# Gate transposes moved to the head of the mLSTM, convolution norm made a step of its own, gate scratch in other buffers

## Chip, core and metric

One NeuronCore of a Trainium2 chip runs the whole program. Its engines are TensorE (PE, with its weight loads as PEld), VectorE (DVE), ScalarE (ACT), GpSimd (POOL) and SyncE (SP), which issues nearly all DMAs. The metric is the device time of one execution in microseconds.

## What is computed

Two layers over 256 latent tokens and 256 context tokens, model width 1024. Each layer has an attention part and an expert part (PEER); the change is in the attention part. Cut to what matters:

```python
h  = rmsnorm(x, norm1_g) * (1.0 + sc1) + sh1          # latent; context with its own modulation
a, mq, mk, mv, mo, mg, dq, dk, dv = split(h @ w_in)
conv  = conv_module(a)         # gate, depthwise convolution of 31 taps, layernorm over 256 channels, silu
mlstm = mlstm_mixer(mq, mk, mv, mo, mg)   # 4 heads, forward and backward, gated by mg
diff  = diff_mixer(dq, dk, dv)            # 4 heads, softmax(q1 k1) - lam * softmax(q2 k2)
x = x + g1 * (concat(conv, mlstm, diff) @ w_out)
x = x + g2 * peer_ffn(rmsnorm(x, norm2_g) * (1.0 + sc2) + sh2)
```

In the second layer the context tokens are needed as keys, values and gates only, so convolution, queries and outputs there cover 256 columns in place of 512.

## The kernel before

The features lie on the 128 partitions and the 512 tokens (context, then latent) on the free axis. `front` (from line 366) is the attention part of a layer, `peer` (from line 889) the expert part. All matrix products are made in three passes: weights and activations are split into a high and a low part. The split of weights (`wsplit`, L228 to L240) loads a block by DMA from SyncE's queue (L232, two buffers), makes the high part on ScalarE (L238) and the low part on GpSimd (L239), 512 columns at a time, into five buffers each.

The order of `front` in the first layer:
- two adaLN halves (`ada_half`, L199), the norm, and the first group projection (`projg`, L331 to L333), which gives the gates, and two blocks of the convolution's input;
- `gate_rows` (L510): on VectorE and ScalarE, logarithm, exponential, splits, cumulative sums (`scan`, L545 and L549) of the gates on 64 partitions. Results: `rows` (L561 to L563), read along the tokens, and ih, il, which are transposed (L569, eight transposes into one PSUM bank of tag "m"), copied to `ah` (L572, VectorE) and exponentiated to `ea` (L573, ScalarE);
- the convolution's gate, the output gates (L407), three late adaLN halves (`late`, L410: accumulators on VectorE, L145 and L147; row products on TensorE, L214; their weights w2 in the buffers kT and qT), the keys, queries and values of the mLSTM (L412 to L419);
- then the steps of `ORDER` (L37), for both layers `kmcvkk0k123`: "k" the keys and queries of one head pair of the differential attention (`keys`, L423, with a rotation through TensorE, L359), "m" the mLSTM (`mlstm`, L595), "c" the convolution with its norm (`conv`, L481), "v" the values of the attention (`values`, L432), digits one head of it (`diff`, L662);
- the output projection, residual and second norm.

`conv` is, for two blocks of 128 channels, one step L486 and thirty steps L489 on VectorE, and then the norm: the mean over 256 channels by two matmuls with ones (L493), VectorE's subtraction (L495), squares and their sum (`sumsq`, L268 and L269), reciprocal root (`rsqrt`, L256 to L261), scale, sigmoid and product (L501 to L506).

The head of `mlstm` spreads a row over the partitions (L611, PSUM tag "m"), and from it makes E by exponentials with bias `ah` on ScalarE (L619), on the diagonal blocks by VectorE's add and minimum with `ah` (L623), an exponential (L625) and GpSimd's triangle (L627); L632 is the product of keys and queries, L637 multiplies it by `ea` and E, L643 is the product with the values.

What sets the order: the program is written in the order told (the traced order). When it is built, a planner lays the instructions out on each engine by its own estimate of durations: among those that it takes to be ready it issues the one traced first, and one traced later may go ahead when the earlier isn't ready yet. On the chip every engine then takes its fixed list in order. `keep_in_program_order` binds an instruction behind the one traced before it on its engine, in order of issue alone. Tiles of one tag share that many buffers as `bufs` says: of the tags here "m" (PSUM) has two, "a" (PSUM) one, "f" (PSUM) three, "PT" two, "v", "vx", "kT" and "qT" one each. "PT" holds the accumulators of the adaLN halves, and later the transposed probabilities of `diff`.

Of the kernel before, what the change touches and what calls it, by code (L numbers as in the profile page):

```python
# [7 lines left out]
F32 = mybir.dt.float32  # L8
# [17 lines left out]
TT = 512  # L26
# [7 lines left out]
LAG = (10, 4)  # L34
HB = 1
LO = ('p', 'p')
ORDER = ('kmcvkk0k123', 'kmcvkk0k123')  # L37
NSUM = 4
MORE = (4, 6)
WB = 5  # L40
# [9 lines left out]
class Net:  # L50
# [315 lines left out]
    def front(self, l, P, c0, late):  # L366

        nc, I, F = self.nc, self.I, self.frontp
        n = TT - c0
# [12 lines left out]
        W = I["w_t"][l]  # L382
        K = self.K = {}
        first = self.projg(I["w_first"][l, 0], h, 0, ("f", "f", "f", "d"))
        rows = self.gate_rows(P, first[0], K)

        vx = K["vx"] = F.tile([128, 4, 4, 128], F32, name="vx", tag="vx")
        for hh in range(4):
# [2 lines left out]
        km = K["km"] = F.tile([128, 2, TT], F32, name="km", tag="km")  # L391
        mq = K["mq"] = F.tile([128, 2, n], F32, name="mq", tag="mq")
        og = K["og"] = F.tile([128, 2, n], F32, name="og")
        v = K["v"] = F.tile([128, 4, 512], F32, name="v", tag="v")
        up = F.tile([128, 2, ns, T + 30], F32, name="up")
        nc.gpsimd.memset(up[:, :, :, 0:15], 0.0)
        nc.gpsimd.memset(up[:, :, :, T + 15:T + 30], 0.0)
# [25 lines left out]
        def keys(b):  # L423
            pk = self.proj(W[BLK_DK + b], h, 0)
            nc.scalar.activation(kT[:, b, :T], pk[:, :T], AF.Copy)
            self.rot(pk[:, T:], kT[:, b, T:])
            pq = self.proj(W[BLK_DQ + b], h, c0)
            if c0 == 0:
                nc.scalar.activation(qT[:, b, :T], pq[:, :T], AF.Copy, scale=0.125)
            self.rot(pq[:, T - c0:TT - c0], qT[:, b, T - c0:], 0.125)  # L430

        def values():  # L432
            for k in range(2):
                for t2, p in enumerate(self.projv(I["w_v"][l, 1 + k], h)):
                    nc.scalar.activation(v[:, 2 * t2:2 * t2 + 2, 256 * k:256 * k + 256], p, AF.Copy)


        seen = 0
        for s in ORDER[l]:
            if s == "m":  # L440
                self.mlstm(P, K, rows, c0)
            elif s == "c":
                cy = self.conv(P, up, n)
            elif s == "v":
                values()
            elif s == "k":
                keys(seen)
                seen += 1
            else:
                self.diff(P, K, int(s), c0)  # L450
# [30 lines left out]
    def conv(self, P, up, n):  # L481
        nc = self.nc
        ys = [self.frontp.tile([128, n], F32, name=f"cy{b}") for b in range(2)]
        for b in range(2):
            y = ys[b].rearrange("p (s t) -> p s t", t=T)
            nc.vector.tensor_scalar(y, up[:, b, :, 0:T], P["conv_w"][:, b, 0:1], P["conv_b"][:, b:b + 1],  # L486
                              op0=OP.mult, op1=OP.add)
            for k in range(1, CONV_K):
                nc.vector.scalar_tensor_tensor(y, up[:, b, :, k:k + T], P["conv_w"][:, b, k:k + 1], y,  # L489
                                         op0=OP.mult, op1=OP.add)  # L490
        mu = self.ps("a")[:, :n]
        for b in range(2):
            nc.tensor.matmul(mu, self.ones, ys[b], start=b == 0, stop=b == 1)  # L493
        for b in range(2):
            nc.vector.scalar_tensor_tensor(ys[b], mu, -1.0 / 256.0, ys[b], op0=OP.mult, op1=OP.add)  # L495
        split = lambda t: t.rearrange("p (s t) -> p s t", t=T)
        yv = [split(y) for y in ys]
        sq, y = (up[:, b, :, 0:T] for b in range(2))
        rs = self.rsqrt(self.sumsq(yv, self.ones, split(self.ps("a")[:, :n]), [sq, y]), 1.0 / 256.0, y, sq)
        for b in range(2):  # L500
            nc.vector.tensor_mul(yv[b], yv[b], rs)  # L501
            nc.vector.tensor_scalar(ys[b], ys[b], P["conv_ln_g"][:, b:b + 1], P["conv_ln_b"][:, b:b + 1],
                                    op0=OP.mult, op1=OP.add)
            sg = self.w(n, "sg", fam="c")
            last = nc.scalar.activation(sg, ys[b], AF.Sigmoid)
            nc.vector.tensor_mul(ys[b], ys[b], sg)  # L506
        self.log_exp(last)
        return ys

    def gate_rows(self, P, ps, K):  # L510

        nc, F = self.nc, self.frontp
        T1 = F.tile([128, 4, TT], F32, name="gr1", tag="v")
        T2 = F.tile([64, 4, TT], F32, name="gr2", tag="vx")
        G = T1[:, 0]
        Fg, e, u = (T1[0:64, k] for k in (1, 2, 3))
        r, L, Bl, M = (T2[:, k] for k in range(4))
        nc.vector.tensor_scalar(G, ps, P["gate_b"][:, 0:1], None, op0=OP.add)
        nc.vector.tensor_copy(Fg, G[64:128])
        ig = G[0:64]  # L520
        nc.scalar.activation(e, Fg, AF.Abs)
        nc.scalar.activation(e, e, AF.Exp, scale=-1.0)
        nc.vector.tensor_scalar(u, e, 1.0, None, op0=OP.add)
        nc.scalar.activation(L, u, AF.Ln)
        nc.vector.tensor_scalar(r, u, -1.0, None, op0=OP.add)
        nc.vector.tensor_sub(r, e, r)
        nc.scalar.activation(u, L, AF.Exp, scale=-1.0)
        nc.vector.tensor_mul(r, r, u)
        nc.vector.tensor_add(L, L, r)
        nc.vector.scalar_tensor_tensor(L, Fg, 0.0, L, op0=OP.min, op1=OP.subtract)  # L530
        lh, ll, ih, il = e, u, r, Fg

        def split(hi, lo, v):
            nc.vector.tensor_scalar(hi, v, SPLIT, None, op0=OP.add)
            nc.vector.tensor_scalar(hi, hi, SPLIT, None, op0=OP.subtract)
            nc.vector.tensor_sub(lo, v, hi)
        split(lh, ll, L)
        split(ih, il, ig)

        def scan(dst, src, op):  # L540
            for d in range(2):
                p = slice(32 * d, 32 * d + 32)
                z = (lambda a: self.zero[p].to_broadcast([32, a.shape[1]])) if op == OP.add else (lambda a: a)
                if d == 0:
                    nc.vector.tensor_tensor_scan(dst[p], src[p], z(src[p]), 0.0, op0=op, op1=op)  # L545
                else:
                    for o, init in ((0, 0.0), (T, dst[p, 0:1])):
                        a = src[p, o:o + T][:, ::-1]
                        nc.vector.tensor_tensor_scan(dst[p, o:o + T][:, ::-1], a, z(a), init, op0=op, op1=op)  # L549
        Bh = L  # L550
        scan(Bh, lh, OP.add)
        scan(Bl, ll, OP.add)
        nc.vector.tensor_sub(ih, ih, Bh)
        nc.vector.tensor_sub(il, il, Bl)
        scan(M, ih, OP.max)
        out = T1[0:64, 2:4]
        nc.vector.tensor_scalar(out[:, 0], M, -1.0, None, op0=OP.mult)
        nc.vector.tensor_add(out[:, 1], Bh, M)
        nc.vector.tensor_add(out[:, 1], out[:, 1], Bl)
        nc.scalar.activation(out[:, 1], out[:, 1], AF.Exp, scale=-1.0)  # L560
        rows = F.tile([128, 2, TT], F32R, name="rows")  # L561
        nc.scalar.activation(rows[:64], out, AF.Copy)
        nc.vector.tensor_sub(rows[64:], out, rows[:64])  # L563
        K["ah"] = F.tile([128, 4, 64], F32, name="ah")
        K["ea"] = F.tile([128, 4, 64], F32, name="ea")
        pt = self.ps("m")
        for k, src in enumerate((ih, il)):
            for tt in range(4):
                nc.tensor.transpose(pt[:, (4 * k + tt) * 64:(4 * k + tt) * 64 + 64],  # L569
                                    src[:, tt * 128:(tt + 1) * 128], self.ident[:64, :64])  # L570
        pv = pt.rearrange("p (k t r) -> p k t r", k=2, t=4)
        nc.vector.tensor_copy(K["ah"], pv[:, 0])  # L572
        nc.scalar.activation(K["ea"], pv[:, 1], AF.Exp)  # L573
        return rows

    def spans(self, i, d, c0):

# [601 lines left out]
```

## Time and profile before

| what | us |
|---|---|
| median of 3 runs | 3153.36 (3150.83 to 3155.54) |
| the profiled execution | 3152.63 |
| its span, first to last instruction | 3150.9 |
| busy: TensorE, weight loads | 2936.4 (93%), 2428.7 (77%) |
| busy: VectorE | 2300.6 (73%) |
| busy: ScalarE, GpSimd | 1443.4 (46%), 1340.1 (43%) |
| mean granted clock of TensorE, share of full speed | 0.971 |

The share of busy time is a mean over stages that have different limits; what a change in one stage is worth is read in that stage. The first attention part lies at about 50 to 403 us of the span, the second at about 2054 to 2290 us. In a line, L569 is line 569 of the kernel, "m<-ident,gr" the tile written and the tiles read, "[8.63 <-DVE gr L553]" idle time of the engine just before, and whose work ended it.

### The profile page before, as it was taken

How to read it: one execution, taken by the hardware profiler on the slowest of the kernel's cores; microseconds unless marked ns; L12 is line 12 of the kernel's file. 1: busy time of each engine (PE TensorE's matmuls, PEld its weight loads, DVE VectorE, ACT ScalarE, POOL GpSimd, SP SyncE). 2: the span in 40 equal slices, each digit the busy share in tenths (PEclk: the TensorE clock that was granted, in tenths of full speed). 3: DMA queues.
4: the chain of work that ended last, by engine and by line, in shares of the span. 5: the costliest groups of instructions: out<-in, count | busy, mean ns of one | idle time of the engine just before them, and what ended most of it. 6: DMA issues, size and time to landing. Idle time of an engine off the chain costs nothing. (4 is left out here: it accounts for less than half of the span.)

```text
span 3150.9 us, 43726 instructions
## 1 busy us (share of the span) xinstructions
PE 2936.4 (93%) x14930; PEld 2428.7 (77%) x14930; DVE 2300.6 (73%) x4819; ACT 1443.4 (46%) x2863; POOL 1340.1 (43%) x1055
## 2 busy tenths in 40 slices
PE   7899989989999998889999999988988899899998
PEld 4476677778888876767888888777787899788887
DVE  7987649977777769997455545586669898766665
ACT  4345443336666632223333333345453666455554
POOL 3334244446666646343434334253466776000000
PEclk9999999999999999999999999999998999999999
DMA  6511123335555587776564645121255677887864
GB/s 223 174 48 54 47 87 115 127 110 201 202 206 204 201 286 247 232 242 198 164 189 152 194 148 173 41 75 60 74 162 162 210 269 261 302 273 250 269 224 139
DMA packets 249807, 550.96 MB, mean 175 GB/s; under 512 B 17440, under 2 KB 118304, under 8 KB 246384
## 3 DMA queue, kind: packets, MB, share of 16 engines
q1 hardware_dynamic: 248864, 545.74, 52.3%
q8 instruction: 118, 1.93, 0.2%
q0 software_dynamic: 720, 2.43, 0.2%
q14 instruction: 105, 0.86, 0.1%
HBM read 456.87 MB, written 91.23 MB: 174 GB/s over the span
## 5 line engine op out<-in xcount | busy, mean ns | idle before, releaser
L863 POOL TENSOR_TENSOR ul<-u,uh 128x512 fp32r<-128x512 f32 x448 | 593.5, 1334 | 433.7 <-ACT uh L862 423.1
L880 PE MATMUL h<-hh,uh 128*128 128x512 f32 (+1 forms) x2048 | 700.1, 342 | 36.1 <-ACT ga L886 34.8
L882 PE MATMUL h<-hh,ul 128*128 128x512 f32 (+1 forms) x2048 | 696.4, 340 | 3.9 <-POOL ul L863 3.9
L881 PE MATMUL h<-hl,uh 128*128 128x512 f32 (+1 forms) x2048 | 697.1, 340 | 0.0
L862 ACT ACTIVATE vh<-v 128x512 fp32r<-128x512 f32 x512 | 319.8, 629 | 573.9 <-PE acc L994 375.6
L862 ACT ACTIVATE uh<-u 128x512 fp32r<-128x512 f32 x512 | 318.8, 628 | 411.9 <-PE h L881 293.5
L863 POOL TENSOR_TENSOR vl<-v,vh 128x512 fp32r<-128x512 f32 x208 | 303.7, 1473 | 365.5 <-ACT vh L862 361.2
L880 PEld LDWEIGHTS h<-hh,uh 128*128 128x128 f32 x2048 | 395.8, 193 | 79.6 <-ACT ga L886 37.4
L882 PEld LDWEIGHTS h<-hh,ul 128*128 128x128 f32 x2048 | 395.2, 193 | 45.9 <-POOL ul L863 4.4
L881 PEld LDWEIGHTS h<-hl,uh 128*128 128x128 f32 x2048 | 395.9, 193 | 38.8
L993 PE MATMUL acc<-vl,wh 128*128 128x512 f32 x1024 | 402.9, 393 | 3.2 <-DVE vl L863 2.9
L992 PE MATMUL acc<-vh,wh 128*128 128x512 f32 x1024 | 402.2, 393 | 3.0 <-ACT vh L862 3.0
L994 PE MATMUL acc<-vh,wl 128*128 128x512 f32 x1024 | 401.4, 392 | 0.0
L831 DVE TENSOR_REDUCE rt_stg<-f 128x256 f32<-128x512 f32 x384 | 243.5, 686 | 142.1 <-PE f L829 141.1
L239 POOL TENSOR_TENSOR wlo<-wt,whi 128x512 fp32r<-128x512 f32 x164 | 242.7, 1491 | 245.3 <-ACT whi L238 217.8
L958 DVE TENSOR_TENSOR ga<-ga,g 128x512 f32<-128x512 f32 x192 | 164.7, 863 | 165.9 <-DMA ga<-act 102.2
L863 DVE TENSOR_TENSOR vl<-v,vh 128x512 fp32r<-128x512 f32 x304 | 208.3, 701 | 105.5 <-ACT vh L862 105.1
L992 PE MATMUL f<-vh,wh 128*128 128x512 f32 x512 | 205.1, 401 | 37.3 <-DVE accS L1000 31.2
L1000 DVE TENSOR_TENSOR accS<-accS,f 128x512 f32<-128x512 f32 x252 | 171.1, 679 | 85.2 <-PE f L994 85.1
L993 PEld LDWEIGHTS acc<-vl,wh 128*128 128x128 f32 x1024 | 194.2, 190 | 46.8 <-DVE vl L863 6.8
L992 PEld LDWEIGHTS acc<-vh,wh 128*128 128x128 f32 x1024 | 193.9, 189 | 43.7 <-ACT vh L862 3.2
L994 PEld LDWEIGHTS acc<-vh,wl 128*128 128x128 f32 x1024 | 193.9, 189 | 40.4
(318 smaller groups left out, 5393.3 us busy)
## 6 DMA issues: line engine op xcount, KB each, us to landing
u<-in_peer_u SPq DMA_DIRECT2D x256, 512.0 KB, 4.0
v<-in_peer_v SPq DMA_DIRECT2D x256, 512.0 KB, 4.4
G<-rt_stg SPq DMA_DIRECT2D x24, 2048.0 KB, 7.0
act<-ga SPq DMA_DIRECT2D x152, 256.0 KB, 2.9
ga<-act SPq DMA_DIRECT2D x152, 256.0 KB, 4.5
g<-G SPq DMA_DIRECT2D x32, 1024.0 KB, 6.1
wa<-in_ada_t SPq DMA_DIRECT2D x56, 512.0 KB, 4.2
w<-in_ada_w SPq DMA_DIRECT2D x20, 1024.0 KB, 6.2
```

The costliest lines, as they stand in the source:

```text
L239: nc.gpsimd.tensor_sub(lo, raw, hi)
L831: nc.vector.tensor_reduce(stg[:, :, t4 + k2:t4 + k2 + 2].rearrange("p j t -> p t j"), pg.rearrange("p (t x j) -> p t j x", t=2, x=2), axis ...
L862: nc.scalar.activation(hi, raw[:, k * 512:(k + 1) * 512], AF.Copy)
L863: lo_eng.tensor_sub(lo, raw[:, k * 512:(k + 1) * 512], hi)
L880: nc.tensor.matmul(o, uh, hh[:, c, c0:], start=c == 0, stop=False)
L881: nc.tensor.matmul(o, uh, hl[:, c, c0:], start=False, stop=False)
L882: nc.tensor.matmul(o, ul, hh[:, c, c0:], start=False, stop=c == NB - 1)
L958: nc.vector.tensor_mul(av, av, g)
L992: nc.tensor.matmul(A, wh[:, t], vh, start=s0 and jj == 0, stop=False)
L993: nc.tensor.matmul(A, wh[:, t], vl, start=False, stop=False)
L994: nc.tensor.matmul(A, wl[:, t], vh, start=False, stop=s1 and jj == 1)
L1000: nc.vector.tensor_add(o, o, A)
```

## The change

- `gate_rows` ends with `rows` and hands back ih and il; their transposes, `ah` and `ea` become a function `gate_cols`, called at the start of the step "m". Each transpose is bound behind what was traced before it on TensorE, so behind the second rotation of the first "k".
- The norm becomes a function `conv_norm` and a step "n" of its own, after "v"; its two matmuls of the mean are bound behind the values' matmuls.
- The scratch of the gates: gr2 (tag "vx", four rows of 512) becomes gr2 and gr3 (tag "PT", two rows each); ih takes the row of Fg and il that of ig, both in gr1 (tag "v"), which so lives until the transposes. The value tile `v` of the attention, of the same tag, is allocated in its step.

```diff
-ORDER = ('kmcvkk0k123', 'kmcvkk0k123')
+ORDER = ('kmcvnkk0k123', 'kmcvnkk0k123')
...
-        rows = self.gate_rows(P, first[0], K)
+        rows, gates = self.gate_rows(P, first[0], K)
...
-        v = K["v"] = F.tile([128, 4, 512], F32, name="v", tag="v")
...
         def values():
+            v = K["v"] = F.tile([128, 4, 512], F32, name="v", tag="v")
...
             if s == "m":
+                self.gate_cols(K, gates)
                 self.mlstm(P, K, rows, c0)
             elif s == "c":
                 cy = self.conv(P, up, n)
+            elif s == "n":
+                self.conv_norm(P, up, n, cy)
...
+        return ys
+
+    def conv_norm(self, P, up, n, ys):
+        nc = self.nc
         mu = self.ps("a")[:, :n]
         for b in range(2):
-            nc.tensor.matmul(mu, self.ones, ys[b], start=b == 0, stop=b == 1)
+            self.tc.keep_in_program_order(nc.tensor.matmul(mu, self.ones, ys[b], start=b == 0, stop=b == 1))
...
-        T2 = F.tile([64, 4, TT], F32, name="gr2", tag="vx")
+        T2, T3 = (F.tile([64, 2, TT], F32, name=k, tag="PT", bufs=2) for k in ("gr2", "gr3"))
...
-        r, L, Bl, M = (T2[:, k] for k in range(4))
+        r, L, Bl, M = T2[:, 0], T2[:, 1], T3[:, 0], T3[:, 1]
...
-        lh, ll, ih, il = e, u, r, Fg
+        lh, ll, ih, il = e, u, Fg, ig
...
+        return rows, (ih, il)
+
+    def gate_cols(self, K, srcs):
+
+        nc, F = self.nc, self.frontp
         K["ah"] = F.tile([128, 4, 64], F32, name="ah")
         K["ea"] = F.tile([128, 4, 64], F32, name="ea")
         pt = self.ps("m")
-        for k, src in enumerate((ih, il)):
+        for k, src in enumerate(srcs):
             for tt in range(4):
-                nc.tensor.transpose(pt[:, (4 * k + tt) * 64:(4 * k + tt) * 64 + 64],
-                                    src[:, tt * 128:(tt + 1) * 128], self.ident[:64, :64])
+                self.tc.keep_in_program_order(
+                    nc.tensor.transpose(pt[:, (4 * k + tt) * 64:(4 * k + tt) * 64 + 64],
+                                        src[:, tt * 128:(tt + 1) * 128], self.ident[:64, :64]))
```

## Rows read from the trace of the kernel before

**Rows 1.** Busy time of each engine by stretch: start:end, length, then each engine.

```profile
core 0: us, PE busy (x) PEld busy (x) DVE busy (x) ACT busy (x) POOL busy (x), PEclk, DMA share, GB/s
76.00:183.50 107.50, 93.03 (x401) 58.77 (x402) 103.60 (x139) 33.35 (x56) 43.98 (x26) 0.95 0.45 152
104.00:110.00 6.00, 5.92 (x15) 2.33 (x16) 5.77 (x10) 0.38 (x1) 0.00 (x0) 0.50 0.11 20
2067.00:2135.60 68.60, 48.99 (x309) 43.30 (x308) 66.90 (x94) 30.80 (x57) 38.74 (x26) 0.89 0.26 85
2094.90:2100.00 5.10, 5.09 (x16) 3.65 (x17) 4.91 (x8) 0.00 (x0) 0.00 (x0) 0.50 0.01 3
2135.60:2142.00 6.40, 6.34 (x28) 5.86 (x28) 2.74 (x9) 2.31 (x7) 2.14 (x3) 0.58 0.01 3
...
183.50:235.00 51.50, 47.69 (x238) 34.97 (x238) 40.23 (x68) 24.36 (x56) 15.16 (x23) 0.90 0.09 31
```

**Rows 2.** TensorE's waits, total, times, longest: 76 to 183, 183 to 403, 2067 to 2142.

```profile
PE m L569 <- DVE gr L553: 8.6, 1, 8.6
...
PE m L632 <- DVE E L623: 1.7, 1, 1.7
...
PE f L349 <- POOL wlo L239: 1.0, 2, 0.7
...
PE m L569 <- DVE gr L553: 11.3, 1, 11.3
PE a L493 <- DVE cy L489: 6.7, 1, 6.7
```

**Rows 3.** VectorE's timeline, first layer: start, length, line, tiles, shapes, count.

```profile
64.55 0.47 DVE L145 TENSOR_SCALAR ada<-w,cc 128x512 f32<-128x512 f32 x1
...
69.06 7.16 DVE L147 SCALAR_TENSOR_TENSOR ada<-w,cc,ada 128x512 f32<-128x512 f32 x6
...
109.72 0.68 DVE L558 TENSOR_TENSOR gr<-gr 64x512 f32<-64x512 f32 x1
...
111.59 2.06 DVE L147 SCALAR_TENSOR_TENSOR ada<-w,cc,ada 128x512 f32<-128x512 f32 x3
```

**Rows 4.** VectorE's timeline around the first masks; last, line L489 from 76 us.

```profile
165.11 18.49 DVE L489 SCALAR_TENSOR_TENSOR cy<-up,small,cy 128x512 f32<-128x512 f32 x17
183.52 0.34 DVE L623 TENSOR_SCALAR E<-m,ah 128x128 f32<-128x128 f32 x1
...
2107.72 27.88 DVE L489 SCALAR_TENSOR_TENSOR cy<-up,small,cy 128x256 f32<-128x256 f32 x43
...
2138.11 0.34 DVE L623 TENSOR_SCALAR E<-m,ah 128x128 f32<-128x128 f32 x1
...
76.00:183.50 107.50, 47.39 (x50) 0.95 0.45 152
```

**Rows 5.** TensorE's timeline around the mLSTM's heads, both layers.

```profile
179.59 0.70 PE L359 MATMUL f<-rp_t,perm 128*128 128x256 f32 x2 [1.88 <-ACT rp_t L357]
...
186.70 1.09 PE L632 MATMUL m<-mq,km 64*128 64x512 f32 x2 [0.96 <-ACT E L625]
...
235.14 1.02 PE L269 MATMUL m<-sq,blk 128*128 128x512 f32 x2
...
2136.67 1.06 PE L359 MATMUL f<-rp_t,perm 128*128 128x256 f32 x2
...
2142.01 0.70 PE L632 MATMUL m<-mq,km 64*128 64x256 f32 x2
```

**Rows 6.** Line L489 in the second layer (duration min/median/max), and GpSimd's timeline.

```profile
L489 DVE SCALAR_TENSOR_TENSOR cy<-up,small,cy x60: 468/476/1591, 2070.0 to 2135.1; 128x256 f32<-128x256 f32 x60
...
95.08 1.32 POOL L239 TENSOR_TENSOR wlo<-wt,whi 128x512 fp32r<-128x512 f32 x1 [1.02 <-ACT whi L238]
111.78 1.07 POOL L390 MEMSET vx<- 128x256 f32 x4 [15.38 <-DVE gr L559]
...
2119.90 8.60 POOL L239 TENSOR_TENSOR wlo<-wt,whi 128x512 fp32r<-128x512 f32 x3 [5.18 <-ACT whi L238]
```

## What the change will do to the time

> **What bounds the kernel now.** The change touches only the two attention fronts (some 76 to 400 us and 2067 to 2286 us of the span), so I read the two fronts and leave the expert stages alone: I take them to move as a whole. First the busy times by stretch: from 76 us to the first mask of the mLSTM at 183.5 us VectorE is busy 103.6 of 107.5 us, and in the second layer, up to the end of the convolution at 2135.6 us, 66.9 of 68.6 us; TensorE has 14 to 20 us less [rows 1]. Then the list of TensorE's waits: 8.6 us at the gate transposes (L569) in the first layer; in the second 11.3 us there and 6.7 us at the mean of the convolution norm (L493) [rows 2]. After each the granted clock is low: 0.50 over 6.0 and over 5.1 us, 0.58 over 6.4 us [rows 1], where 0.50 is the 1.2 GHz level; the half lost is 3.0, 2.5 and 2.7 us. So the three stalls cost 26.7 + 8.2 = 34.9 us of TensorE time. Last come the timelines of VectorE and TensorE around both heads of the mLSTM, for the order of their lists. The question is whether that is TensorE's to gain. All three end on VectorE, and VectorE has hardly a gap. Behind the heads of the two mLSTMs it is the other way round (183.5 to 235 us: TensorE 47.7, VectorE 40.2 of 51.5 us [rows 1]), so time is counted there by TensorE.
>
> **The planner's lag.** TensorE takes its list in order. That it stood 11.3 us at L569 means that the list was laid out as if VectorE would be that much further on. The same happens again at L493. A pair of transposes moved later meets the same late VectorE at the next place where TensorE needs something new of it.
>
> **Part 1, transposes at the head of the mLSTM.** It takes the waits of 8.6 and 11.3 us off L569: the gate rows are ready at about 110 us [rows 3], and the new place is behind keys(0), which ends at about 180 us. No instruction is added: 8 transposes, one copy to ah, one exponential to ea per layer, as before. But the masks (L623) and exponentials (L619) take their bias from ah, so now nothing of the mLSTM starts on VectorE or ScalarE before VectorE has come to the ah copy in its list; and the bank "m" has two buffers, of which the transposes hold one until ah and ea are read, so the second L611 waits too, and TensorE with it, with all value projections queued behind.
> Where is that copy in VectorE's list? In the second layer 43 convolution steps (L489) run through from 2107.7 to 2135.6 us, and the first mask comes only after them [rows 4]. The planner had thus finished the convolution by the end of the first key projection, when L611 was issued; the copy will be due later still (behind the second projection of keys(0) and its rotation). So all 60 steps stand ahead of it. In the first layer 17 steps run in one piece until 183.5 us, and 50 of the 60 lie ahead of the first mask [rows 4], so ten behind it; but the copy is due some 8 us of TensorE later than that mask was: rotation and 24 matmuls 6.1 us (179.6 to 186.7, less 1.0 of wait [rows 5]), the second rotation 0.7, the transposes about 1. In that time the list can take up some or all of those ten.
> So the stall moves to the heads. What a head's start must be, to leave the total as it is, I work out by TensorE's remaining work.
> Second layer: before, TensorE spends 2136.7 to 2142.0 on the rotation and the 24 matmuls, and 0.6 on the second rotation: 5.9 us [rows 5] that will lie ahead of the stall. Against it stand 0.4 for L611, the slow clock after a stall, 2.5, and 1.0 (an estimate: one mask and one exponential of 0.34 us each, and hand-overs). Saved: 2.0 us. Break-even is a head at 2135.7 + 2.0 = 2137.7 us.
> First layer: from 183.5 us to the norm of the first two heads at 235.1 us TensorE takes 51.6 us [rows 4, 5]. Off go waits of 1.7 and about 0.7 at L349 [rows 2] and 1.0 at L632 [rows 5], the rest of the 24 matmuls (183.5 to 185.7, where the row of L632 has 1.0 us of wait ahead of it) and a rotation of 0.7: 6.3; on come 2.5 + 1.0. 48.8 us are left: break-even is a head at 235.1 - 48.8 = 186.3 us.
>
> **Part 2, gate scratch.** gr2 and gr3 take the two buffers "PT", which the adaLN accumulators (ada) use before and after. I take buffers of one tag to be given out in traced order. Then the accumulator of the first late adaLN half can't start before the gate rows have let go of gr2, at L558, 109.7 us [rows 3]. In the kernel before, its first eight steps (two L145, six L147) run from 64.6 to 76.2 us, while VectorE has little else [rows 3]. They now come into the full stretch: 8 x 0.69 = 5.5 us (L147 runs three in 2.06 us at 111.6 us). Bounds 0 (buffers given to whoever asks first) and 5.5; I take 5.5. Their two weight buffers (kT, qT) come free later too, and SyncE's loads of the next chunks with them, so TensorE may stop at an L214 about where it stopped at L569; this lies ahead of the head and I give it no price of its own. GpSimd's memset of vx no longer waits 15.4 us for gr2 [rows 6]; TensorE stood in that time anyway. The value tile v, now allocated in its step, waits for transposes that are traced ahead of it: nothing.
>
> **Part 3, the norm later.** L493 with its 6.7 us stands behind the value projections, where the convolution is long done: that wait goes. So do 2.7 us of slow clock; both go into the stall at the head, whose end is set by the same steps L489. Some 8 us (first layer) of norm work on VectorE move out of the first two heads into a stretch with gaps; TensorE is dense in both: nothing.
>
> **VectorE and GpSimd.** One step L489 takes 0.468 us at best and 1.591 us at worst in the second layer; three splits of weights on GpSimd take 8.60 us beside it, where one alone takes 1.32 us [rows 6]. The two slow each other. Since TensorE will have used the weights of the second key projection before the head, I expect two more splits ahead of it. Bounds 0 and 2 x (1.591 - 0.468) = 2.2 us a layer; I take 2.2, since GpSimd's list isn't held up by the stall. The Trainium skill (SBUF — State Buffer, Who interferes with whom) says that a VectorE instruction with two SBUF inputs, as L489 has, and a GpSimd instruction that reads SBUF shut each other out for a whole instruction. By it the two splits would cost 2 x 1.32 = 2.6 us a layer, and the total would be 0.8 us higher; the rows agree as to its direction.
>
> **Sum.** First layer: 183.5 + 5.5 (ada) + 2.1 (3 of the ten steps at 0.69: room for 12 in 8 us, of which the 8 ada steps and a rotation take up 9) + 0.8 (rotation) + 2.2 - 3.9 (VectorE's gaps, filled) = 190.2 us, 3.9 us later than break-even. Bounds: 180.4 (no ada, no steps, no splits) to 200.6 (all ten steps, 6.9, three splits at 1.3, no gap filled): 5.9 faster to 14.3 slower. Second layer: 2135.7 + 0.8 + 2.2 - 1.0 (of 1.7 us gaps) = 2137.7 us: 0. Bounds 2134.7 to 2140.3: 3.0 faster to 2.6 slower. Together 3.9 us slower, bounds 8.9 faster and 16.9 slower. The profiled execution takes 3152.63 us, 0.7 us less than the median of the runs: 3156.5, and by the median **3157 us**, its own range 3145 to 3167.
>
> **Rivals.** *The stalls are gone and not paid again* (faster). If the copy to ah and the masks stand in VectorE's list ahead of the rest of the convolution, TensorE loses neither. For it: the mLSTM is traced ahead of the convolution, and masks do interrupt it in the first layer [rows 4]. Against: the 43 steps in one piece. Price: first layer 8.6 + 3.0 = 11.6, second 11.3 + 2.5 + 6.7 + 2.7 = 23.2. Most likely in one layer only: 3130 for the second, 3142 for the first, 3118 for both.
> *VectorE is made later by the moved scratch* (slower): the eight ada steps and all ten convolution steps come ahead of the first layer's copy. It decides once that head starts later than 186.3 + 6.3 = 192.6 us; at 200.6 us it costs 14.3, with 2.6 of the second layer: 3169 us.
> *The change has no effect*: other waits hold the same engines at the same places. 3153 us.
>
> **How the numbers follow.** A measurement of this kernel tells about 0.2%, 6.3 us, from no change: 3147.1 to 3159.7 is "same". Forecast 0.47 (same 0.37, slower 0.10); stalls gone 0.27, all faster; scratch 0.18, all slower; no effect 0.08. Faster 0.27, same 0.45, slower 0.28. Range 3128 to 3169: below it lies the case of both layers gained (about 0.1), above it 0.08.
>
> **What would show it.** In the profile after: L569 without a wait on the gate rows, but a wait on TensorE of over 10 us at the heads (L611, or the first L632) that VectorE's ah copy ends; 60 steps L489 ahead of that copy in the second layer, 53 or more in the first; L145 of the first late half after 109 us; L493 without a wait. I am wrong if TensorE passes the heads with less than 5 us of wait, or if the copy to ah stands ahead of the last dozen steps L489.

## Result and profile after

| | median | lowest to highest |
|---|---|---|
| before | 3154.45 us | 3150.83 to 3159.64 |
| after | 3178.14 us | 3171.96 to 3180.44 |

The ratio is 1.0071, 95% interval 1.0055 to 1.0088: the change costs 0.7%, some 22 to 24 us. I had said 3157 us and a range up to 3169. The profiled execution of after took 3171.96 us (span 3170.2, granted clock 0.964 against 0.971).

Where the time went is read from TensorE's busy time and clock in five stretches of the first layer's front. The stretches run from the first gate-row instruction of VectorE to the first L611 (L622 after), from there to the product behind the first heads that spreads a gate row for their division (first L650, after L661), to that behind the second heads (third L650), to the last attention product (last L695, after L706), and to the first product of the second norm's sum of squares (L475, after L478). Columns: start:end, length, TensorE's busy time, granted clock, DMA share, GB/s. First before:

```profile
76.20:176.20 100.00, 87.61 (x380) 0.95 0.45 154
176.20:220.60 44.40, 39.80 (x158) 0.88 0.10 33
220.60:269.20 48.60, 47.52 (x245) 1.00 0.20 65
269.20:360.20 91.00, 83.59 (x337) 1.00 0.11 35
360.20:377.60 17.40, 14.88 (x62) 1.00 0.24 68
2067.00:2128.10 61.10, 48.17 (x306) 0.89 0.23 76
2128.10:2163.50 35.40, 28.63 (x152) 0.90 0.15 49
2163.50:2276.90 113.40, 104.71 (x570) 0.97 0.21 66
```

The last three rows are the second layer (its second and last heads in one). The same stretches of after:

```profile
73.50:189.20 115.70, 97.49 (x419) 0.93 0.43 146
189.20:224.80 35.60, 33.49 (x174) 0.95 0.09 31
224.80:283.40 58.60, 51.23 (x205) 0.88 0.12 36
283.40:383.60 100.20, 93.84 (x328) 0.88 0.10 32
383.60:401.30 17.70, 15.29 (x64) 1.00 0.25 68
2083.60:2157.40 73.80, 55.89 (x333) 0.84 0.27 86
2157.40:2180.90 23.50, 23.47 (x133) 0.93 0.01 2
2180.90:2295.80 114.90, 105.85 (x563) 0.97 0.20 65
```

A row splits into three: idle time is length less busy time; what the clock takes is length times (1 - granted clock), since at 0.50, the 1.2 GHz level, half the time is lost; the rest is work. In the first layer the front grows from 301.4 to 327.8 us, 26.4. Idle time is 8.5 of that, the clock 18.6, and the work is slightly less (-0.7). By stretch:

- up to the head: 15.7 longer, of which 6.8 is work that was done behind the head before; with the first heads (8.8 shorter) it is 6.9 longer. The front also begins 2.7 us earlier, so the first heads end 4.2 later;
- **second heads: 10.0 longer** (idle 1.1 to 7.4, clock 0 to 7.0, less work);
- **last heads: 9.2 longer**, all of it the clock (0 to 12.0).

The second layer's front grows by 2.3 us. The expert stage between the fronts is 7.1 us shorter in this execution (0.6 and 2.8 in two later ones of after), the one behind them 0.4 longer: -2.7 + 26.4 - 7.1 + 2.3 + 0.4 = 19.3 us of span.

TensorE's waits of after (total, times, longest): first 73 to 225 us, then 225 to 384, then 2083.6 to 2181.

```profile
PE a L214 <- DMA w<-in_ada_w: 13.4, 2, 11.8
PE m L622 <- ACT ea L585: 2.0, 1, 2.0
...
PE m L643 <- DVE E L634: 5.7, 1, 5.7
PE m L702 <- DVE df_p L699: 3.3, 1, 3.3
PE d L689 <- ACT df_p L693: 1.7, 3, 1.3
...
PE f L348 <- ACT km L411: 10.9, 1, 10.9
```

The transposes (L581) and the norm's mean (L500) stand in none of them: the three waits of [rows 2] are gone. TensorE stands 11.8 us at the weights of the late adaLN instead. SyncE issued their load at 113.27 us only, after it had itself waited for VectorE's last step (L147) on the buffer:

```profile
SPq L208 <- DVE ada L147: 18.8, 3, 12.7
```

In the second layer TensorE stands 10.9 us at a value projection, whose bank waits for the copy of km. It hardly stands at the heads: 2.0 us at the second L622. In the second heads there is a new wait of 5.7 us. What holds it is read from ScalarE's timeline there (start, length, line, operation, tiles):

```profile
256.82 1.28 ACT L512 ACT_TABLE_LOAD   x1
258.12 0.63 ACT L512 ACTIVATE sg<-cy 128x512 f32<-128x512 f32 x1
258.77 0.60 ACT L657 ACTIVATE ml_dab<-m 64x512 f32<-64x512 f32 x1
259.38 0.59 ACT L658 ACTIVATE ml_nu<-m 64x512 f32<-64x512 f32 x1
259.99 1.28 ACT L630 ACT_TABLE_LOAD   x1
261.28 0.95 ACT L630 ACTIVATE E<-m,ah 128x384 f32<-128x384 f32 x2
262.25 1.28 ACT L512 ACT_TABLE_LOAD   x1
263.54 0.63 ACT L512 ACTIVATE sg<-cy 128x512 f32<-128x512 f32 x1
264.19 1.28 ACT L636 ACT_TABLE_LOAD   x1
265.49 0.31 ACT L636 ACTIVATE E<-E 128x128 f32<-128x128 f32 x1
...
267.45 1.28 ACT L246 ACT_TABLE_LOAD   x1
```

The norm's two sigmoids (L512) stand among the exponentials of the mLSTM (L630, L636). Each change between the two functions loads a table, four times, and the kernel's own load behind the norm (L246) is a fifth: five loads of 1.28 us within 12 us, in which ScalarE has no gap. TensorE's 5.7 us, for a bank whose readers are these exponentials and masks, end at 268.28 us, behind four of the five.

### The profile page after: what moved, and what is told of

Read it like the earlier page. It is cut to its first block, busy times and chain, and to the rows that moved or that the text cites. A ratio compares the mean times of both kernels' runs of the same rounds, so it can differ in the third digit from the quotient of the medians.

```text
span 3170.2 us, 43719 instructions
## 1 busy us (share of the span) xinstructions
PE 2955.4 (93%) x14930; PEld 2441.1 (77%) x14930; DVE 2292.0 (72%) x4819; ACT 1441.8 (45%) x2863; POOL 1332.7 (42%) x1055
## 5 line engine op out<-in xcount | busy, mean ns | idle before, releaser
L874 DVE TENSOR_TENSOR vl<-v,vh 128x512 fp32r<-128x512 f32 x304 | 208.2, 702 | 106.8 <-ACT vh L873 106.6
```

Source lines behind the costliest of these rows:

```text
L874: lo_eng.tensor_sub(lo, raw[:, k * 512:(k + 1) * 512], hi)
```

## Experiments

The theories at the start: N, the norm's new place is the loss; S, the scratch in PT is; and a third, that the transposes at the head are the loss themselves (G).

**The parts singly and in pairs.** The norm put back, its two matmuls no longer bound (transposes at the head and scratch in PT stay):

```diff
-ORDER = ('kmcvnkk0k123', 'kmcvnkk0k123')
+ORDER = ('kmcvkk0k123', 'kmcvkk0k123')
...
                 cy = self.conv(P, up, n)
+                self.conv_norm(P, up, n, cy)
```

> The changed kernel, but the convolution norm stands where it stood before (traced right behind the convolution, free to be placed by the planner); gate transposes at the head and scratch in PT stay. Theory N (the norm step is the loss: its two sigmoids change ScalarE's table between the exponentials of the second heads, and TensorE waits for a mask there): the 11.7 us of the second heads in the first layer come back, and the low clock over 323 to 350 us, if it follows from them: 3178 - 12 - 10 = 3156 us, or 3166 if the low clock stays; the wait at the norm's mean in the second layer (6.7 us before) may return. Theory S (the scratch in PT is the loss, the norm costs nothing): no change within 6 us of 3178; the low clock over 323 to 350 us is still there.

The norm alone, as a pinned step of the kernel before:

> The kernel before, with only the norm made a step of its own behind the first value projection and its two matmuls pinned; gate transposes and scratch as before. Theory N: the second heads of the first layer take some 12 us longer, with five table loads between the exponentials, and the low clock follows; the second layer gains the wait at the mean with its slow clock, 9.4 us: 3154 + 12 + 10 - 9 = 3167 us, or 3157 without the low clock. Theory S: the norm costs nothing in the first layer and gains 9.4 in the second: 3145 us.

The changed kernel with its scratch as before:

```diff
-        T2, T3 = (F.tile([64, 2, TT], F32, name=k, tag="PT", bufs=2) for k in ("gr2", "gr3"))
+        T2 = F.tile([64, 4, TT], F32, name="gr2", tag="vx")
...
```

> The changed kernel, but the gate scratch lies in vx's buffer as before; the two rows that the transposes read stay in the buffer of v, so that vx comes free as before. Theory S: the eight steps of the late adaLN run before 76 us again, TensorE's wait of 11.8 us at the adaLN matmuls goes, VectorE comes to the ah copy some 5.5 us earlier: 3178 - 5 = 3173 us if the norm's loss stays. If the 11.8 us are a loss of their own, not given back at the head: 3166 us. Theory N: the wait moves from the adaLN matmuls to the head, 3172 to 3178 us.

The transposes at the head alone (both edits; the two rows that the transposes read stay in gr1):

> The kernel before with only the gate transposes moved to the head of the mLSTM (scratch in vx's buffer, norm as before). By the prediction's sum without its part on the scratch: first layer's head at 190.2 - 5.5 = 184.7 us, 1.6 us before break-even, second layer 0: 3152 us. Theory N (all that is lost comes from the norm step): 3145 to 3155 us. A rival, by which the transposes at the head are themselves the loss (masks and exponentials of both head pairs all late, ScalarE's queue fuller): over 3165 us.

And, with e9 and e10 below, the scratch alone (the transposes called right behind gate_rows, not pinned):

> The kernel before with only the gate scratch moved into the buffers PT; transposes right behind the gate rows, norm as before. Theory S: the first eight steps of the late adaLN come behind the gate rows (111 us), 5.5 us of VectorE in the full stretch; TensorE stops at the adaLN weights as well as at the transposes, or in their place: 3156 + 4 to 3156 + 10 us. Rival (buffers are no matter when TensorE waits at the transposes anyway): 3153 to 3158 us.

Measured, with the lengths of the first layer's stretches from each one's profile:

| | ratio to before (95%) | to the head | first heads | second heads | last heads |
|---|---|---|---|---|---|
| before | 1 | 100.0 | 44.4 | 48.6 | 91.0 |
| transposes | 1.0035 (1.0021 to 1.0049) | 117.5 | 45.0 | 48.6 | 85.9 |
| norm | 1.0060 (1.0043 to 1.0077) | 99.7 | 41.7 | 58.4 | 107.6 |
| scratch | 1.0000 (0.9986 to 1.0015) | 102.8 | 42.9 | 54.1 | 92.6 |
| transposes, scratch | 1.0059 (1.0044 to 1.0074) | 115.8 | 38.9 | 51.9 | 98.5 |
| transposes, norm | 1.0087 (1.0070 to 1.0104) | 118.1 | 34.4 | 59.8 | 100.1 |
| all three (after) | 1.0071 (1.0055 to 1.0088) | 115.7 | 35.6 | 58.6 | 100.2 |

None of the three theories holds alone. The norm costs 0.6% by itself and the transposes 0.35%; together 0.87%, close to the sum. The scratch costs nothing by itself; beside the transposes alone it goes with a loss of 0.24%, beside both with a gain of 0.16%, neither much more than the intervals. With the scratch in PT the costs don't add: putting the norm back takes the changed kernel from 1.0071 to 1.0059 only, less than the intervals, where theory N had 3156 or 3166 us (median 3175.82). The norm and the scratch without the transposes were not run. The column of the second heads gives the norm's place: 58.4 to 59.8 us with it there, 48.6 to 54.1 without; it is worth 9.8 us there in the kernel before and 6.7 in the changed one. The column up to the head gives the transposes: 115.7 to 118.1 with them, 99.7 to 102.8 without.

TensorE's waits from 76 us on in the kernel with the transposes alone:

```profile
PE a L156 <- DVE ada L147: 10.7, 1, 10.7
PE m L623 <- ACT ea L586: 4.3, 1, 4.3
```

The scratch isn't needed for a stall in the late adaLN: with it at its old place TensorE stands 10.7 us at an instruction there that needs VectorE (L156). The 8.6 us of L569 went to a later meeting of TensorE with VectorE, and grew. The head came later than in after, too. The copy to ah, first with the transposes alone, then in after:

```profile
198.68 0.42 DVE L585 COPY ah<-m 128x256 f32<-128x256 f32 x1
```

```profile
191.64 0.42 DVE L584 COPY ah<-m 128x256 f32<-128x256 f32 x1
```

59 convolution steps stand ahead of the first, 52 ahead of the second.

In the kernel with the norm alone the second layer didn't gain. Up to the end of the second heads' mLSTM (third L650) it is 5.8 us shorter (121.8 us in place of 127.6); from there to the last attention product, where the norm now lies, it is 8.0 longer: 2.1 idle, 3.3 clock, 2.7 work that moved there. First before, then the norm alone:

```profile
2194.58:2262.18 67.60, 63.72 (x311) 0.97 0.18 56
```

```profile
2211.76:2287.37 75.61, 69.66 (x326) 0.93 0.20 56
```

**Table or place?** The norm stays in its new place, but its sigmoid is made from functions that need no other table:

```diff
-            last = nc.scalar.activation(sg, ys[b], AF.Sigmoid)
+            nc.scalar.activation(sg, ys[b], AF.Exp, scale=-1.0)
+            nc.vector.tensor_scalar(sg, sg, 1.0, None, op0=OP.add)
+            nc.scalar.activation(sg, sg, AF.Ln)
+            nc.scalar.activation(sg, sg, AF.Exp, scale=-1.0)
             nc.vector.tensor_mul(ys[b], ys[b], sg)
-        self.log_exp(last)
```

> The changed kernel, with the norm in the same place, but y*sigmoid(y) worked out as y*exp(-ln(1+exp(-y))): three instructions on ScalarE of 0.6 us each and one more on VectorE in place of a sigmoid, and no table load among the exponentials. Theory T (the loss in the second heads of the first layer is ScalarE's table, five loads of 1.28 us, and the low clock after TensorE's wait for them): second heads 58.6 -> about 50 us, 3178 - 8 = 3170 us, with the low level over 323 to 350 us as before. Rival P (the place: ten VectorE steps of the norm between the masks make TensorE wait, whatever ScalarE does): second heads stay at 57 to 60 us, 3178 us.

Ratio 1.0050 (1.0031 to 1.0069), not clear of the 1.0071 of after; what the edit does is read from its stretch. Its second heads, and TensorE's wait in them:

```profile
223.80:275.60 51.80, 49.21 (x209) 0.93 0.14 41
```

```profile
PE m L645 <- DVE E L636: 1.3, 1, 1.3
```

The place is the same, 5.7 us of wait are 1.3, and 58.6 us are 51.8: of the 10.0 us the tables are 6.8. With the norm put back it was 51.9, so the other 3.2 us aren't owed to its place. The last heads lost 13.3 us of clock (102.0 us at 0.87), as after lost 12.0. The same edit on the kernel before, where it had little to win:

> The kernel before, with the same exponential form of the sigmoid in the norm and nothing else. There the norm's loads stand in the first heads (222 us) and behind them in the second layer (2153 us). Theory T: up to two switches of 2.6 us a layer go, of which the trace shows no TensorE wait at that place: 3150 to 3156 us. Rival: the order of the lists shifts and brings the low level into the last heads: over 3162 us.

1.0024 (1.0005 to 1.0042): a little slower. Where the loads stood before, the trace had no wait of TensorE on them, and nothing was gained by taking them out. The rival's time came (median 3167.55 us); its reason isn't in the profiled execution (3158.66 us), whose last heads lost 1.8 us of clock.

**What stands ahead of what in VectorE's list.** The convolution steps held back (`ah_copy` is the copy to ah, `first_masks` the last mask of the first two heads):

```diff
             for k in range(1, CONV_K):
+                with self.tc.issue_after((self.first_masks if b and k > 10 else self.ah_copy).ins):
                     nc.vector.scalar_tensor_tensor(y, up[:, b, :, k:k + T], ...
```

> The kernel before, with the convolution steps held back on VectorE: each stands behind the ah copy, and the last twenty of a layer behind the masks of the first two heads. Theory L (TensorE's waits at the gate transposes are convolution steps standing ahead of the gate chain in VectorE's list, and every wait that is taken away there comes back unless the steps go behind the heads): L569 without a wait in both layers, none in its place, 3156 - 11.6 - 13.8 = 3131 us. Rival H (work held back past the head is paid in the heads and at the norm's mean, where VectorE has 11 us of gaps only): 3150 to 3160 us, a wait of over 8 us at the mean or at the first masks.

1.0013 (0.9998 to 1.0027). Theory L is refuted: TensorE's waits at the transposes stay, here 7.6 us in the first layer and 10.2 in the second:

```profile
PE m L570 <- DVE gr L554: 7.6, 1, 7.6
```

That nothing is gained is nearer to rival H, but its wait of over 8 us at the mean or the first masks didn't come either (2.8 and 5.9 us at the mean).

So the convolution wasn't what kept the gate rows. Without one step L489 ahead of it the ah copy comes at 106.8 us in place of 108.9: the gate chain has 27 instructions of its own on VectorE up to there, and where the steps are gone it waits for ScalarE. What the twenty steps held back give in the first layer's first heads (44.4 to 37.5 us) they take in the second heads (48.6 to 57.3). The same on the changed kernel, for the last twenty steps alone:

> The changed kernel, with the last twenty convolution steps of each layer put behind the masks of the first two heads on VectorE. Theory L: the ah copy of the second layer has 40 steps ahead of it and not 60 and comes some 13 us earlier, that of the first layer some 8 us; but TensorE's waits that lie ahead of the head (11.8 us at the late adaLN, 10.9 us at the value projection) are not touched, so that only the head's own 2 to 5 us go: 3172 to 3178 us. Rival H (the head is what holds the changed kernel): 3160 us.

1.0039 (1.0021 to 1.0057). 40 steps stand ahead of each ah copy, 52 and 60 in the changed kernel. The first heads of the first layer shrink to 31.8 us, the second layer's front to 205.4 (212.2 after, 209.9 before). The waits ahead of the heads stay (11.9 and 10.9 us), as theory L said; the gain is larger than it said, though (3169.46 us, where it had 3172 to 3178). Why is not shown. Both repairs together:

> The changed kernel with both repairs: the last twenty convolution steps behind the first masks, and the sigmoid of the norm by exponentials. Each alone took the ratio to the kernel before from 1.0071 to 1.0039 and to 1.0050. If the two gains add (theory A): ratio 1.0018, some 3161 us, second heads of the first layer under 52 us. Rival: the low level in the last heads of the first layer stays (13 us of clock lost there with either) and takes up what the second heads gain: 1.004, 3168 us.

1.0037 (1.0019 to 1.0054): they don't add. With the steps held back, the norm's sigmoid comes at 279 us, behind the second heads' exponentials, so there is nothing left for the other form to save.

**The low clock in the last heads.** In after, from 328 to 349 us, TensorE is busy all the time and gets the 1.2 GHz level:

```profile
320.00:328.00 8.00, 6.65 (x19) 1.00 0.03 14
328.00:349.00 21.00, 21.00 (x45) 0.51 0.00 0
```

Ahead of it stands a wait of 1.30 us for an exponential, which had waited 3.13 us for a row maximum that stood behind low halves (hl) in VectorE's list. These were given to GpSimd:

```diff
-            nc.vector.tensor_sub(hl[:, c, c0:], t, hh[:, c, c0:])
+            (nc.gpsimd if c < 4 else nc.vector).tensor_sub(hl[:, c, c0:], t, hh[:, c, c0:])
```

> The changed kernel, with the low halves (hl) of the four blocks cy and og, ahead of the out-projection, made by GpSimd in place of VectorE. In the changed kernel two of them stand ahead of the row maximum (df_mx) for which ScalarE's exponential waits 3.13 us, TensorE then waits 1.30 us for that exponential, and its granted clock is low for the next 20 us. Theory W (this wait is what leads to the low level): the 1.30 us go under 0.5 and with them the low level over 323 to 350 us: 3178 - 11 = 3167 us. Rival C (the low level comes from what went on before, the wait has nothing to do with it): the low stretch of 20 us stays, 3177 us.

1.0073 (1.0047 to 1.0098), no gain, and neither expectation fits whole. The wait at the scores is 0.2 us, but there are new ones at L702, 6.9 us in two where after had one of 3.3, and the clock is low for a shorter time:

```profile
283.40:378.50 95.10, 85.77 (x326) 0.93 0.11 34
```

6.7 us of clock in place of 12.0, with 3.0 more of idle time. That this wait decides the level is not shown. So the changed kernel and the one before were profiled again:

> The changed kernel once more, for a second trace. If the low level in the last heads of the first layer belongs to the list (theory B): again 20 us at 0.50 behind a wait of 1.3 us at the scores, 12 us of clock lost between the second heads and the last product. If it falls by chance (theory C): 0 to 7 us lost there, and the span is shorter by as much.

> The changed kernel, for a third trace. Theory B: 12 us of clock lost in the last heads, as in the first trace. Theory C: something between 0 and 12, not the same as in the second.

> The kernel before, for a second trace. Theory B: its last heads run at full clock again, as in its first trace. Theory C: they lose 5 to 10 us of clock in some executions, as the first layer of the kernel with the second layer changed did (6.8).

The last heads, in the second and third execution of after and the second of before:

```profile
280.90:381.00 100.10, 93.69 (x326) 0.88 0.11 32
```

```profile
285.00:385.00 100.00, 93.61 (x327) 0.88 0.11 32
```

```profile
266.80:366.70 99.90, 92.43 (x337) 0.90 0.12 34
```

Each theory is right on one kernel: B on after, which loses 12.0 us in all three profiled executions, C on before. Before lost nothing in the first and 10.0 us in the second, by the same list of instructions, behind the same wait: it stood at L691 for 1.49 us in the first and 1.54 in the second, and what follows are these rows, first from the first execution, then from the second:

```profile
313.62 0.44 PE L691 MATMUL m<-ident,df_p 128*128 128x128 f32 x2 [1.49 <-DVE df_p L688]
...
317.44 1.13 PE L695 MATMUL m<-df_PT,v 128*128 128x256 f32 x4
```

```profile
311.19 0.44 PE L691 MATMUL m<-ident,df_p 128*128 128x128 f32 x2 [1.54 <-DVE df_p L688]
...
317.32 2.07 PE L695 MATMUL m<-df_PT,v 128*128 128x256 f32 x4
```

The products run at the full clock in one and at half in the other. Whether the level falls behind a wait of a microsecond and a half isn't settled by the wait. So the 9.2 us of the last heads are a cost of the change only against those executions of before that kept the clock. What makes after lose it each time stays open. Over all kernels profiled here, this stretch lost 10.2 to 13.5 us of clock with the norm in its new place (6.7 with hl on GpSimd), and 0 to 11.8 with it in the old one: the norm's place goes with the loss, but doesn't decide it.

**The half that gained.** The transposes at the head in the second layer only, with its last twenty convolution steps behind the first masks; first layer, norm and scratch as before:

> The kernel before in the first layer; in the second the gate transposes at the head of the mLSTM (scratch in vx's buffer, norm as before) and the last twenty convolution steps behind the masks of the first two heads. If the layers' parts stand for themselves (theory A: the second layer's front gained 4.6 us with the transposes moved alone, and 6.8 us with the last twenty steps held back on top of the whole change; the first layer alone lost): first layer's front 301 us as before, second 198 to 205 in place of 210: 3147 to 3152 us where before has 3155. Rival: the gain of one stretch is given back in the heads or the last heads of the same layer: 3153 to 3160 us.

0.9985 (0.9968 to 1.0001); medians 3154.42 against 3160.17 us. The second layer's front took 204.6 us against 209.9, as theory A says. The first layer's lists are in effect those of before, and up to the last heads each stretch is within 0.8 us of it; the last heads lost 6.8 us of clock in its profiled execution, as those of before lost 10.0 in the second. It is better than after, by intervals that don't meet. That it is better than before is not shown: the interval reaches 1, and the first four executions of before had the same median (3154.45 us).

## Why the prediction was wrong, step by step

**The lag.** "A pair of transposes moved later meets the same late VectorE at the next place where TensorE needs something new of it." This held, with 11.8, 10.7 and 10.9 us where before had 8.6 and 11.3. Why VectorE is late I had wrong in part: I took it for a list full of convolution steps, but with these held back the waits are still 7.6 and 10.2 us. The gate chain itself takes VectorE up to 106.8 us.

**The place of the stall.** I put it at the heads, over 10 us, and it was 2.0 there. The next place was the late adaLN, and in the second layer ScalarE: its exponential of the gate rows (L566) waited 13.15 us for VectorE with the copy of km behind it in the list, and TensorE behind that:

```profile
2120.61 0.63 ACT L566 ACTIVATE gr<-gr 64x512 f32<-64x512 f32 x1 [13.15 <-DVE gr L565]
2121.15 0.57 ACT L411 ACTIVATE km<-f 128x512 f32<-128x512 f32 x1
```

I had searched TensorE's list for its next need of VectorE, and not ScalarE's. The stop at L214 I saw, but gave it "no price of its own".

**The size of the first stretch.** The ah copy of the first layer came at 191.6 us (190.2 forecast), the first heads ended 4.2 us later than in before's first execution (3.9 forecast; 1.6 and 5.2 in the second and third execution of after, and each 2.5 more against before's second). In part this is luck. Without the scratch the same sum gives 190.2 - 5.5 = 184.7 us, and the transposes alone brought the copy at 198.7, 14 us later, with 59 steps ahead of it; they cost 0.35% where the sum had nothing. The scratch, which was to add 5.5 us, went with an earlier copy: 192.15 us with both. So a head that was put too early and a scratch term of the wrong sign made up for each other.

60 convolution steps stand ahead of the copy in the second layer, 52 in the first (I had asked for 53). The second layer's front was forecast at 0. It takes 212.2, 211.0 and 212.0 us in three executions, against 209.9 and 211.2 in the two of before. That balance hides two terms I had wrong in the second layer. GpSimd's two splits, 2.2 us (2.6 by the rule of the Trainium skill, SBUF — State Buffer, Who interferes with whom), came ahead of the copy, but behind the last convolution step: 22 splits stand ahead of its end in either kernel, which lies 68.7 us behind the first gate instruction, 68.6 before. So no run here shows what two more beside it would cost. The copy came 74.6 us behind that instruction and not 70.7, held by TensorE and no longer by VectorE.

**Part 2.** The first L145 of the late half came at 111.00 us, as said. Eight ada steps in the full stretch were to cost 5.5 us; the scratch alone measures 1.0000. What I left out is that six of these steps (L147) stood right ahead of the gate chain: without them the front begins 3.6 us earlier with the scratch alone (2.7 to 4.5 in the three executions of after), and its first stretch is 2.7 us longer.

**Part 3 is the step that failed.** "Some 8 us of norm work on VectorE move out of the first two heads into a stretch with gaps; TensorE is dense in both: nothing." I counted VectorE's instructions and not ScalarE's: the norm has two sigmoids, and the new place is among exponentials. The second heads grew by 10.0 us, 6.8 of them the table loads, and the norm alone costs 0.6% in all. The Trainium skill ("ScalarE: Activation LUTs", Table sets: the hidden batching unit) says to do all functions of one table set before changing to another, which would have warned me. Its price for a change (same page, What ACT_TABLE_LOAD costs), a load of 1.28 us and a drain of 1.38, 2.66 together, isn't what these rows show: the load is 1.28 us, and the function starts 1.29 to 1.30 us after the load does.

**The norm's mean.** L500 has no wait, as said. The 9.4 us of the second layer's stall and clock were to go into the stall at the head. With the norm alone 5.8 us were gained up to the end of the second heads, and 8.0 were lost behind it.

**The clock.** I took 2.5 us for a slow clock after a stall, from three stalls of 7 to 11 us. In after 12.0 us of it stand behind a wait of 1.3 us. None of my cases had a term for the last heads. In the profiled execution this (9.2 us) and the second heads (10.0 us) are what Part 3 and the clock had at nothing, and most of what carried the time beyond the range.

**The rivals.** "Stalls gone" and "no effect" didn't come. "Scratch later" had the right sign for another reason: the first layer's copy came at 191.6, short of the 192.6 us from which it decides. Its price has a slip: 14.3 + 2.6 us on the median of 3153.36 are 3170 us and not 3169; the measured 3178 lies beyond both.

## What to carry to other kernels

When a step is moved, walk through the lists of all engines at the new place, not only of the one that was full at the old: a function that changes ScalarE's table costs a load there and one back for each time it stands among others. A wait on an engine that is late by its own chain wasn't removed here by moving the one who waits; look for the next instruction that needs it, on third engines too. Where TensorE waits a little more than a microsecond in a dense stretch, set a range for the clock as well, and take a second profile before a clock loss is put down to a change.

## What I had not expected of the hardware

The 1.2 GHz level lasted some 20 us in after's last heads, although TensorE was busy for all of the 21.00 us shown. After the longer stalls it had lasted 5.1 to 6.4 us [rows 1]. The same list with the same wait of 1.5 us ran at 1.00 in one execution and lost 10.0 us of clock in the next.
